# Replacing a seven-product feed-forward by plain three-product matmuls of 512 columns, with one weight pool from the RWKV readout on

## The chip, the cores and the metric

The kernel runs on one core of a Trainium2 chip, as one launch. The metric is the device time of that launch in microseconds. TensorE is called PE below, its weight loads PEld, VectorE DVE, ScalarE ACT, GpSimd POOL, and SP is the engine that issues the DMAs.

## What is computed

The reference is a network of two blocks over 512 latent tokens and 256 context tokens of 1024 features. The first block has an attention and delta-net layer and a Hyena layer; the second has an attention layer and an RWKV layer, each followed by a SwiGLU feed-forward. The change touches the feed-forward behind the RWKV layer, which is the last step before the final norm. By then only the 512 latent tokens are left:

```python
def _swiglu(h, wg, wu, wd):
    return (jax.nn.silu(h @ wg) * (h @ wu)) @ wd
...
        h2 = _rmsnorm(x, norm2_g[i]) * (1.0 + m[:, 4]) + m[:, 3]
        x = x + m[:, 5] * _swiglu(h2, ffn_wg[i], ffn_wu[i], ffn_wd[i])
...
    return _rmsnorm(x, final_g)
```

`wg` and `wu` are 1024 x 2816 and `wd` is 2816 x 1024: in units of 128 features, 8 columns in, 22 columns hidden, 8 columns out.

## The kernel before

All activations are held feature-major: `self.x` is eight tiles of 128 features by 512 tokens. A float32 factor is split into a high and a low part in a rounded format (`hi`, a copy by ACT; `lo`, the difference, on POOL or DVE), and a float32 product is made of three matmuls, high by high, high by low and low by high, which add up in one PSUM bank (`mm3`, L189 to L193).

**The plain scheme** is `linear` (L195). It makes 128 output features: `load_w` (L178) has SP load one slab of the weights (`wraw`, two buffers), ACT makes `whi` (L172) and POOL makes `wlo` (L168; three buffers each), and per chunk of 128 of the contraction `mm3` issues its three matmuls. A column of `wg` or `wu` has 8 chunks, so 24 matmuls. The first feed-forward (`ffn`, L1482 onwards) uses it for 512 latent and 256 context tokens side by side: for each hidden column a column of `wg` and one of `wu`, Silu on ACT (L1507), the product on DVE (L1511), and the split of the result on ACT and POOL; the hidden columns come in groups of 8, 8 and 6, and after each group eight columns of `wd` add what it gives to `x` (`residual`, L1321). The eight output columns of the RWKV readout (`rwkv_out`) use `linear` for the latent tokens alone.

**The seven-product scheme** is `ffn_s` (L381). It takes weights and activations as 2 x 2 blocks and forms two output columns by 512 tokens from seven block products of 256 columns in place of eight, as in Winograd's form of Strassen's multiplication. `strassen` (L314) loads two slabs (L326), forms sums and differences of weight blocks on DVE (`total`, L336, four a call), splits seven blocks (`form`, L291 on ACT and L292 on POOL or DVE), runs the seven products, and combines them from PSUM on DVE (L359, L362, L363, L366) with one copy on ACT (L352). `sums` (L304) forms and splits the sums of activation blocks (L310 to L312). The first pair of columns goes by eight products (`eight`, L367) while the sums of the inputs are still being made. The hidden pairs come in groups of 4, 6, 6 and 6 columns, and the `wd` columns of a group are issued behind the first pair of the next.

**Around it.** `rwkv_out` ends with the eight columns of `rw_wo`; each adds to `x` and counts its squares (L232 on ACT, L234 on DVE, and behind the last column two matmuls L236), and behind the eighth the norm factor `r` follows on ACT (L209, L210). The feed-forward begins with that factor. `finish` scales `x` by the last norm factor (L2036 on ACT, L2037 on DVE and POOL) and stores eight tiles (L2038).

What sets the order: at build time a planner lays out the instructions of each engine by program order and by its own estimate of when operands and buffers are ready, and each engine and each DMA queue then works in that fixed order. A tile waits until all readers of the tile that held its space are done. The weight pool `w1` of the readout is closed before the feed-forward opens its own pools in the same space, which hold 176 KB per partition. `norm_mod` (L246) is the plain scheme's norm: per chunk a product on DVE (L255), the high part on ACT (L262), the shifted value on DVE (L263) and the low part on POOL (L168).

```python
        nc.tensor.matmul(ps, lhsT=a[0], rhs=b[0], start=start, stop=False)
        nc.tensor.matmul(ps, lhsT=a[0], rhs=b[1], start=False, stop=False)
        nc.tensor.matmul(ps, lhsT=a[1], rhs=b[0], start=False, stop=stop)
```

Of the kernel before, what the change touches and what calls it, by code (L numbers as in the profile page):

```python
# [10 lines left out]
F32 = mybir.dt.float32  # L11
# [6 lines left out]
L = 512  # L18
C = 256

# name -> number of 128-feature columns
# [17 lines left out]
_FFG = [[8, 8, 6], [4, 6, 6, 6]]  # L39
# [13 lines left out]
def nat_i(ap):  # L53
    """(column, row) tokens, seen as (row, column)."""
    return ap.rearrange("p (c r) -> p r c", r=8)
# [6 lines left out]
class K:  # L62
# [38 lines left out]
    @contextmanager  # L101
    def phase(self, name, side="left", **tags):
        """tag -> (bufs, columns); the enclosing phases' tags stay."""
        outer = getattr(self, "pb", None), getattr(self, "tags", {})
        with self.tc.tile_pool(name=name, bufs=1, side=side, reuse_waits="tile") as self.pb:
            self.tags = {**outer[1], **{t: (self.pb, *n) for t, n in tags.items()}}
            yield
        self.pb, self.tags = outer

    @contextmanager  # L110
    def psum(self, name, **tags):
        """tag -> bufs, or (bufs, banks)."""
# [13 lines left out]
    def halves(self, name, dt=F32):  # L126
        """an endless supply of [128, 256], two to a tile."""
        while True:
            t = self.k2(name, dt)
            yield t[:, 0:256]  # L130
            yield t[:, 256:512]
# [26 lines left out]
    def table(self, i):  # L158
        """loads an activation table; ScalarE's instructions of the block stay behind it."""
# [6 lines left out]
    def ptt(self, out, in0, in1, op):  # L166
        """a tensor_tensor on GpSimd."""
        self.nc.gpsimd.tensor_tensor(out=out, in0=in0, in1=in1, op=op)  # L168

    def split(self, src, hi, lo, psum=False):  # L170
        """float32 = hi + lo, both in the rounded format."""
# [23 lines left out]
    def linear(self, src, acts, evac, kc=8, late=False, w=None):  # L195
        """128 outputs. acts: list of (list of (hi, lo) per K chunk, n); evac(a, psum)."""
# [7 lines left out]
    def rstd(self, ps, n, scale, eps, name="rstd", bias=0.0, table=False, out=None):  # L204
        """exp(bias) (ps scale + eps)^-1/2"""
# [7 lines left out]
    def sumsq(self, tiles, n):  # L213
        """tiles: [128, 512], 512 / n chunks each; -> sums over all of them, on all partitions."""
# [10 lines left out]
    def count(self, key, c, src, n, scale=1.0, tag="ss"):  # L225
        """adds the squares of column c of 8; -> their sum with the last one."""
# [12 lines left out]
    def squares(self, a, c, n, tag="ss"):  # L239
        """counts column c in the norms of x (a = 0) or ctx; with the last one they are in self.rr[a]."""  # L240
# [4 lines left out]
    def norm_mod(self, tiles, n, g, sh, name, table=False, tag="k2", r=None):  # L245
        """(x rstd) g + sh, split; g, sh: [128, 8] columns."""  # L246
# [28 lines left out]
    def mod(self, w, chunks, outs):  # L275
        """outs: list of (silu(c) rows, out columns tile, chunks below which it is wanted)."""
# [12 lines left out]
    def split_on(self, vector, src, hi, lo):  # L289
        """split, the difference on VectorE or GpSimd."""  # L290
        self.nc.scalar.copy(hi, src)  # L291
        (self.nc.vector if vector else self.nc.gpsimd).tensor_tensor(out=lo, in0=src, in1=hi.bitcast(F32), op=ALU.subtract)  # L292
        return hi, lo

    def operand(self, ts, n, tag):
        """ts: [128, 4 n] each, the blocks 22 11 21 12 of right operands' chunks: rows of the first | second half of the
        contraction, columns of the first | second half of the tokens. -> the split factors of the seven products."""
        hl = [[self.sb(tag, tag + x, F32R)[:, :7 * n] for x in "hl"] for _ in ts]
        for t, (h, l) in zip(ts, hl):
            self.split_on(False, t[:, :3 * n], h[:, 0:3 * n], l[:, 0:3 * n])  # L300
        return self.sums(ts, n, hl)

    def sums(self, ts, n, hl):
        nc = self.nc  # L304
        tt = nc.vector.tensor_tensor
        for t, (h, l) in zip(ts, hl):
            s = self.sb("sT", "sT")[:, :4 * n]
            b = t.rearrange("p (a n) -> p a n", a=4)
            # T1 | T3, T2 | -T4
            tt(out=s[:, 0:2 * n].rearrange("p (a n) -> p a n", a=2), in0=b[:, ::-3], in1=b[:, 1::2], op=ALU.subtract)  # L310
            tt(out=s[:, 2 * n:3 * n], in0=t[:, 0:n], in1=s[:, 0:n], op=ALU.subtract)
            tt(out=s[:, 3 * n:4 * n], in0=t[:, 2 * n:3 * n], in1=s[:, 2 * n:3 * n], op=ALU.subtract)  # L312
            self.split_on(True, s[:, 0:2 * n], h[:, 3 * n:5 * n], l[:, 3 * n:5 * n])
            self.split_on(False, s[:, 2 * n:], h[:, 5 * n:], l[:, 5 * n:])  # L314
        return [{k: (h[:, i * n:i * n + n], l[:, i * n:i * n + n]) for i, k in enumerate(("22", "11", "21", "T1", "T3", "T2", "T4"))} for h, l in hl]

    def strassen(self, srcs, acts, n, kc=8, plain=False):
        """2 x 128 outputs (srcs: their columns of the weights), 2 n tokens, seven products for eight (Winograd's form).
        acts: operand() per chunk of half the contraction; -> [128, 4 n], blocks in the order of operand()."""
        nc = self.nc  # L320
        m = kc // 2
        w = 128 * m
        raw = []
        for src in srcs:
            raw.append(self.sb("wr", "wraw"))
            nc.sync.dma_start(raw[-1][:, :2 * w], src)  # L326
        A = {f"{i + 1}{j + 1}": raw[i][:, j * w:j * w + w] for i in range(2) for j in range(2)}

        def form(k, vector):
            hi, lo = (self.sb("w" + x, "w" + x, F32R)[:, :w] for x in ("fh", "fl"))  # L330
            self.split_on(vector, A[k], hi, lo)
            return [t.rearrange("p (k m) -> p k m", k=m) for t in (hi, lo)]

        def total(k, a, b, op, out=None):
            A[k] = A[out] if out else self.sb("ws", "wsum")[:, :w]
            nc.vector.tensor_tensor(out=A[k], in0=A[a], in1=A[b], op=op)  # L336

        def product(ps, a, b, vector=False):
            f = form(a, vector)
            for k in range(m):  # L340
                self.mm3(ps, [t[:, k, :] for t in f], acts[k][b], k == 0, k == m - 1)

        if plain:
            return self.eight(form, acts, n)
        p1 = self.bank("mm", "pst")[:, :n]
        x, y, z = (self.bank("mm", "pst")[:, :2 * n].rearrange("p (a n) -> p a n", a=2) for _ in range(3))
        o = self.sb("so", "so")[:, :4 * n]
        o4 = o.rearrange("p (a n) -> p a n", a=4)
        tt = nc.vector.tensor_tensor
        bc = lambda t: t.unsqueeze(1).to_broadcast([128, 2, n])  # L350
        product(p1, "11", "11")
        nc.scalar.copy(o4[:, 1], p1)  # L352
        total("S1", "21", "22", ALU.add)
        total("S3", "11", "21", ALU.subtract, "21")
        total("S2", "S1", "11", ALU.subtract, "11")
        product(x[:, 1], "12", "21")
        total("S4", "12", "S2", ALU.subtract, "12")
        product(x[:, 0], "S2", "T2")
        tt(out=o4[:, 0:2], in0=x, in1=bc(o4[:, 1]), op=ALU.add)  # L359
        product(y[:, 1], "S1", "T1", True)  # L360
        product(y[:, 0], "S3", "T3")
        tt(out=o4[:, 2:4], in0=y, in1=bc(o4[:, 0]), op=ALU.add)  # L362
        tt(out=o4[:, 0], in0=y[:, 1], in1=o4[:, 2], op=ALU.add)  # L363
        product(z[:, 1], "S4", "22")
        product(z[:, 0], "22", "T4")
        tt(out=o4[:, 2:4], in0=z, in1=o4[:, 2:4], op=ALU.add)  # L366
        return o  # L367

    def eight(self, form, acts, n):
        """strassen() by the eight products."""  # L370
        o = self.sb("so", "so")[:, :4 * n]
        o4 = o.rearrange("p (a n) -> p a n", a=4)
        f = {k: form(k, k[0] == k[1]) for k in ("11", "12", "21", "22")}
        for slot, i, j in ((1, 1, 1), (2, 2, 1), (0, 2, 2), (3, 1, 2)):
            ps = self.bank("mm", "pst")[:, :n]
            for q in (1, 2):
                for k, a in enumerate(acts):
                    self.mm3(ps, [t[:, k, :] for t in f[f"{i}{q}"]], a[f"{q}{j}"], q == 1 and k == 0, q == 2 and k == len(acts) - 1)
            self.nc.scalar.copy(o4[:, slot], ps)
        return o  # L380

    def ffn_s(self, i, ml, mc, g, groups):
        """the same for x alone, seven products for eight."""
        nc, A = self.nc, self.A
        n = 256
        ts, hl = [], []
        for c in range(4):
            t = self.sb("sh", "nm")[:, :1024]
            h, l = (self.sb("sx", "sx" + x, F32R) for x in "hl")
            b, hb = (a.rearrange("p (a n) -> p a n", n=n) for a in (t, h))  # L390
            ts.append(t)
            hl.append((h, l))
# [1897 lines left out]
```

## Time and profile before

| what | value |
|---|---|
| times of three runs | 3710.51, 3719.08 and 3720.9 us |
| median of the runs | 3719.08 us |
| profiled execution, first to last instruction | 3710.4 us |
| mean granted TensorE clock over it | 0.912 of full speed |
| PE, DVE, POOL, ACT busy over it | 85%, 66%, 55%, 42% |
| last feed-forward: first to last matmul start | 3235.5 to 3690.2 us |
| first feed-forward, dense part | 1661.6 to 2190 us |

The profiled execution is as long as the fastest of the three runs, to 0.1 us; the median stands 8.6 us above it. Times in the trace count from the first instruction. A share of busy time is a mean over stages that have different limits, so that the stage of the change is read by itself. PEclk is the granted clock: 1.00 is 2.4 GHz and 0.50 is 1.2 GHz. The duration of a matmul includes its passage through the array; how often one starts is read from the starts of neighbours.

### The profile page before, as it was taken

Reading aid. Unit: us, or ns where it says so; the run is one execution under the profiler, and the core shown is the slowest. Engines: PE = TensorE matmul, PEld = TensorE weight load, DVE = VectorE, ACT = ScalarE, POOL = GpSimd, SP = SyncE. Lnnn points to the kernel's source line nnn. Section 1 sums busy time; section 2 is a strip of 40 time slices with the busy share of each in tenths; the row PEclk is TensorE's granted clock in tenths of the full one; section 3 lists DMA queues with packets and bytes.
Section 4 is the critical chain, followed back from the end, with each engine's and each line's share of the span. In section 5 each row is a group of like instructions: output and inputs, shape, how many; then the busy total and the mean of one; then the engine's idle time right before and its main releaser. Section 6 shows DMA issues by size and latency. Waiting matters only on the chain. (4 is left out here: it accounts for less than half of the span.)

```text
span 3710.4 us, 56859 instructions
## 1 busy us (share of the span) xinstructions
PE 3144.4 (85%) x21442; PEld 2555.7 (69%) x21442; DVE 2457.0 (66%) x3749; ACT 1547.8 (42%) x3033; POOL 2050.1 (55%) x1855
## 2 busy tenths in 40 slices
PE   5678896889997889999999996898667787788887
PEld 1257675767876677778888885666556666488886
DVE  7977844547775676570532339565788885689987
ACT  3347542443222456632121133563545554343434
POOL 6742531446665555434333336467468871488886
PEclk9889996999998899999999997799778988899998
DMA  6312358733441431032343421454322324212221
GB/s 212 119 63 80 134 196 242 211 122 124 134 139 44 130 103 35 19 125 63 114 148 114 136 86 59 163 211 146 96 61 78 81 75 126 83 57 83 83 86 63
DMA packets 266633, 412.37 MB, mean 111 GB/s; under 512 B 73844, under 2 KB 155380, under 8 KB 266360
## 3 DMA queue, kind: packets, MB, share of 16 engines
q1 hardware_dynamic: 266360, 408.75, 35.1%
q8 instruction: 169, 2.77, 0.3%
q14 instruction: 104, 0.85, 0.1%
HBM read 331.34 MB, written 70.25 MB: 108 GB/s over the span
## 5 line engine op out<-in xcount | busy, mean ns | idle before, releaser
L168 POOL TENSOR_TENSOR wlo<-wraw,whi 128x1024 fp32r<-128x1024 f32 (+1 forms) x204 | 506.3, 2484 | 728.1 <-ACT whi L172 705.5
L172 ACT CAST whi<-wraw 128x1024 fp32r<-128x1024 f32 (+1 forms) x204 | 211.5, 1039 | 606.3 <-PE pmm L192 504.4
L191 PE MATMUL pmm<-hxh,whi 128*128 128x512 f32 x968 | 391.7, 406 | 11.2 <-ACT hxh L262 6.5
L192 PE MATMUL pmm<-hxl,whi 128*128 128x512 f32 x968 | 389.1, 402 | 13.2 <-POOL hxl L168 13.2
L284 DVE SCALAR_TENSOR_TENSOR mjunk<-mraw,cv 128x1024 bf16<-128x1024 f32 x224 | 358.7, 1601 | 61.6 <-DMA mraw<-in_mod_w 36.9
L193 PE MATMUL pmm<-hxh,wlo 128*128 128x512 f32 x968 | 387.6, 401 | 0.0
L292 POOL TENSOR_TENSOR wfl<-wraw,wfh 128x512 fp32r<-128x512 f32 (+2 forms) x220 | 306.4, 1422 | 83.8 <-ACT wfh L291 79.9
L191 PE MATMUL pmm<-hch,whi 128*128 128x256 f32 x760 | 222.0, 292 | 9.4 <-ACT hch L262 6.7
L192 PE MATMUL pmm<-hcl,whi 128*128 128x256 f32 x760 | 221.5, 291 | 8.1 <-POOL hcl L168 8.0
L192 PEld LDWEIGHTS pmm<-hxl,whi 128*128 128x128 f32 x968 | 184.1, 190 | 57.4 <-POOL hxl L168 18.8
L191 PEld LDWEIGHTS pmm<-hxh,whi 128*128 128x128 f32 x968 | 184.3, 191 | 53.9 <-ACT hxh L262 9.0
L193 PE MATMUL pmm<-hch,wlo 128*128 128x256 f32 x760 | 221.2, 291 | 0.0
L193 PEld LDWEIGHTS pmm<-hxh,wlo 128*128 128x128 f32 x968 | 184.2, 190 | 40.9 <-issue 0.7
L914 POOL TENSOR_TENSOR X<-X,binv 128x30 f32<-128x30 f32 (+4 forms) x330 | 195.9, 594 | 23.7
L913 POOL TENSOR_TENSOR binv<-X 128x30 f32<-128x30 f32 (+4 forms) x330 | 192.4, 584 | 24.0
L193 PE MATMUL pst<-sxh,wfl 128*128 128x256 f32 x608 | 182.4, 302 | 27.1 <-POOL wfl L292 16.7
L191 PE MATMUL pst<-sxh,wfh 128*128 128x256 f32 x608 | 181.5, 299 | 11.5 <-ACT wfh L291 11.2
L192 PE MATMUL pst<-sxl,wfh 128*128 128x256 f32 x608 | 178.8, 294 | 3.4 <-POOL sxl L398 3.4
L291 ACT CAST wfh<-wraw 128x512 fp32r<-128x512 f32 (+2 forms) x224 | 117.8, 560 | 150.9 <-DVE wraw L336 126.0
L191 PE MATMUL pmm<-lh,whi 128*128 128x512 f32 (+1 forms) x360 | 134.0, 378 | 38.6 <-ACT lh L1579 19.1
L191 PEld LDWEIGHTS pmm<-hch,whi 128*128 128x128 f32 x760 | 149.0, 196 | 18.3 <-ACT hch L262 8.5
L192 PEld LDWEIGHTS pmm<-hcl,whi 128*128 128x128 f32 x760 | 148.8, 196 | 16.8 <-POOL hcl L168 11.6
(599 smaller groups left out, 9288.4 us busy)
## 6 DMA issues: line engine op xcount, KB each, us to landing
mraw<-in_mod_w SPq DMA_DIRECT2D x96, 512.0 KB, 3.6
wraw<-in_wg SPq DMA_DIRECT2D x44, 512.0 KB, 3.6
wraw<-in_wu SPq DMA_DIRECT2D x44, 512.0 KB, 3.6
wraw<-in_e_w_in SPq DMA_DIRECT2D x32, 512.0 KB, 3.8
wraw<-in_o_w_in SPq DMA_DIRECT2D x32, 512.0 KB, 3.5
mraw<-in_e_mod_w SPq DMA_DIRECT2D x24, 512.0 KB, 4.0
mraw<-in_o_mod_w SPq DMA_DIRECT2D x24, 512.0 KB, 4.1
wraw<-in_wd SPq DMA_DIRECT2D x32, 384.0 KB, 3.1
```

Source lines behind the costliest of these rows:

```text
L168: self.nc.gpsimd.tensor_tensor(out=out, in0=in0, in1=in1, op=op)
L172: self.nc.scalar.copy(hi, src)
L191: nc.tensor.matmul(ps, lhsT=a[0], rhs=b[0], start=start, stop=False)
L192: nc.tensor.matmul(ps, lhsT=a[0], rhs=b[1], start=False, stop=False)
L193: nc.tensor.matmul(ps, lhsT=a[1], rhs=b[0], start=False, stop=stop)
L284: nc.vector.scalar_tensor_tensor(out=junk, in0=raw, scalar=1.0, in1=cv, op0=ALU.mult, op1=ALU.mult, accum_out=out[:, c:c + 1])
L291: self.nc.scalar.copy(hi, src)
L292: (self.nc.vector if vector else self.nc.gpsimd).tensor_tensor(out=lo, in0=src, in1=hi.bitcast(F32), op=ALU.subtract)
L913: tt(out=tv, in0=v[:, k + 1:, k:k + 1].to_broadcast(sh), in1=v[:, k:k + 1, :k].to_broadcast(sh), op=ALU.mult)
L914: tt(out=v[:, k + 1:, :k], in0=v[:, k + 1:, :k], in1=tv, op=ALU.add)
```

## The change

The second feed-forward is computed by `ffn`, the function of the first, called with the latent tokens alone: `ffn(1, ...)` leaves the context out of `acts`. The functions of the seven-product scheme go. The hidden columns of the second feed-forward are grouped 8, 8, 6 instead of 4, 6, 6, 6. The pool `w1`, opened for the readout's weights, stays open until the end and also holds the feed-forward's `wraw`, `whi` and `wlo`. The feed-forward's other tiles come from 52 buffers of 512 columns (104 KB per partition), and it has six PSUM banks for products instead of seven. The diff also removes comments and docstrings, which moves the line numbers.

```diff
-_FFG = [[8, 8, 6], [4, 6, 6, 6]]
+_FFG = [[8, 8, 6], [8, 8, 6]]
...
-    def split_on(self, vector, src, hi, lo):
...
-    def operand(self, ts, n, tag):
...
-    def sums(self, ts, n, hl):
...
-    def strassen(self, srcs, acts, n, kc=8, plain=False):
...
-    def eight(self, form, acts, n):
...
-    def ffn_s(self, i, ml, mc, g, groups):
...
-                self.linear(A[f"wd0{gi}"][c], [(hid[a], n) for a, (_, n) in enumerate(acts)], dev, kc=nf, late=True)
+                self.linear(A[f"wd{i}{gi}"][c], [(hid[a], n) for a, (_, n) in enumerate(acts)], dev, kc=nf, late=True)
...
-            t = self.sb("sx", "fin")[:, :L]
+            t = self.k2("fin")
...
-    with k.weights("w1"), k.phase("ro", "right", ld=(16, 512)), k.phase("rc", "right", k2=(40, 512)), k.psum("ps_out", mm=2, pp=2, p=3, ss=1):
-        k.rwkv_out(m[0])
-    with k.phase("f1", k2=(2, 512), ws=(2, 512), sT=(1, 1024), so=(3, 1024), sx=(8, 1792), sh=(8, 1792), wr=(4, 1024), wfh=(6, 512), wfl=(6, 512)), k.psum("ps_f1", mm=7, ss=1):
-        k.ffn_s(1, *m, _FFG[1])
-        k.finish(out)
+    with k.weights("w1"):
+        with k.phase("ro", "right", ld=(16, 512)), k.phase("rc", "right", k2=(40, 512)), k.psum("ps_out", mm=2, pp=2, p=3, ss=1):
+            k.rwkv_out(m[0])
+        with k.phase("f1", k2=(52, 512)), k.psum("ps_f1", mm=6, ss=1):
+            k.ffn(1, *m)
+            k.finish(out)
```

## Rows read from the trace of the kernel before

**Rows 1.** Busy us (instructions) by engine, clock, DMA share, GB/s: the last feed-forward.
```profile
3235.00:3692.00 457.00, 388.80 (x2796) 368.30 (x2796) 410.88 (x447) 191.75 (x380) 363.64 (x254) 0.91 0.24 73
```

**Rows 2.** PE's timeline, the last 256-column matmuls: start, duration.
```profile
3690.11 0.28 PE L192 MATMUL pst<-shl,wfh 128*128 128x256 f32 x1
3690.23 0.28 PE L193 MATMUL pst<-shh,wfl 128*128 128x256 f32 x1
```

**Rows 3.** Waits, 3262 to 3692: total us, times, longest.
```profile
ACT wfh L291 <- DVE wraw L336: 126.0, 34, 7.8
POOL wfl L292 <- ACT wfh L291: 59.9, 43, 4.1
...
PEld pst L193 <- POOL wfl L292: 25.9, 37, 2.0
```

**Rows 4.** DVE's timeline, residuals of two neighbouring columns of the readout.
```profile
3212.68 0.75 DVE L1321 SCALAR_TENSOR_TENSOR x<-pmm,ml,x 128x512 f32<-128x512 f32 x1 [1.70 <-PE pmm L193]
...
3218.26 0.75 DVE L1321 SCALAR_TENSOR_TENSOR x<-pmm,ml,x 128x512 f32<-128x512 f32 x1 [1.68 <-PE pmm L193]
```

**Rows 5.** As rows 1: the first feed-forward, dense part.
```profile
1661.60:1700.00 38.40, 38.40 (x205) 33.26 (x205) 9.65 (x17) 14.53 (x21) 25.44 (x16) 0.95 0.14 43
1700.00:2190.00 490.00, 489.98 (x2787) 427.82 (x2786) 155.84 (x217) 99.92 (x145) 184.53 (x99) 1.00 0.35 113
```

**Rows 6.** DMA issues of the page: count, KB each, median us to landing.
```profile
wraw<-in_wg SPq DMA_DIRECT2D x44, 512.0 KB, 3.6
...
wraw<-in_wd SPq DMA_DIRECT2D x32, 384.0 KB, 3.1
```

**Rows 7.** Costliest groups, 1700 to 2190: busy us, mean ns, idle before.
```profile
L168 POOL TENSOR_TENSOR wlo<-wraw,whi 128x1024 fp32r<-128x1024 f32 x53 | 133.8, 2524 | 253.3 <-ACT whi L172 253.3
...
L172 ACT CAST whi<-wraw 128x1024 fp32r<-128x1024 f32 x53 | 55.6, 1049 | 281.6 <-PE pmm L192 256.8 <-DMA wraw<-in_wu 23.6 <-DMA wraw<-in_wg 1.1
...
L168 POOL TENSOR_TENSOR hl<-sg,hh 128x512 fp32r<-128x512 f32 x20 | 25.8, 1292 | 1.6 <-ACT hh L172 1.6
...
L1511 DVE TENSOR_TENSOR sg<-sg,pmm 128x512 f32<-128x512 f32 x20 | 13.8, 688 | 93.6 <-PE pmm L193 92.5 <-ACT sg L1507 1.1
L172 ACT CAST hh<-sg 128x512 fp32r<-128x512 f32 x20 | 12.4, 621 | 4.4 <-DVE sg L1511 4.1
L1507 ACT ACTIVATE sg<-pmm 128x512 f32<-128x512 f32 x20 | 11.9, 593 | 0.0
```

**Rows 8.** ACT's timeline, the last squares of the readout and its norm factor.
```profile
3230.20 0.63 ACT L232 ACTIVATE sq<-x 128x512 f32<-128x512 f32 x1 [4.94 <-DVE x L1321]
...
3232.86 0.63 ACT L210 ACTIVATE r<-r 128x512 f32<-128x512 f32 x1
```

**Rows 9.** DVE and ACT timelines, the norm of the first feed-forward, two chunks.
```profile
1658.44 0.68 DVE L255 TENSOR_TENSOR nm<-x,r 128x512 f32<-128x512 f32 x1
...
1659.16 0.81 ACT L262 ACTIVATE hxh<-nm,ml,gx 128x512 fp32r<-128x512 f32 x1 [1.12 <-DVE nm L255]
...
1660.46 0.68 DVE L255 TENSOR_TENSOR nm<-x,r 128x512 f32<-128x512 f32 x1
```

**Rows 10.** As rows 1: the last feed-forward's first 26.5 us.
```profile
3235.50:3262.00 26.50, 15.12 (x60) 13.36 (x61) 25.86 (x26) 10.83 (x20) 19.16 (x12) 0.51 0.20 60
```

**Rows 11.** DVE's timeline, the final products at the end of the kernel.
```profile
3700.41 5.83 DVE L2037 TENSOR_TENSOR fin<-fin,r 128x512 f32<-128x512 f32 x6 [5.25 <-ACT r L210]
```

**Rows 12.** PE's timeline, the last matmul of the readout's last column.
```profile
3228.98 0.40 PE L193 MATMUL pmm<-roh,wlo 128*128 128x512 f32 x1
```

**Rows 13.** SP's timeline, the first weight loads of the last feed-forward.
```profile
3228.71 0.80 SPq L326 DMA_DIRECT2D wraw<-in_wg  x2
```

**Rows 14.** PE's waits in the readout, 3180 to 3230: total us, times, longest.
```profile
PE pmm L191 <- ACT roh L172: 2.7, 1, 2.7
PE pmm L192 <- POOL rol L168: 1.0, 1, 1.0
PE pmm L191 <- DVE x L1321: 0.3, 1, 0.3
```

More of the change, by code (lines that the diff above doesn't have):

```diff
@@ L287, in mod_tile @@
         return (pool or self.pm).tile([128, n], F32, name=name)
-    def split_on(self, vector, src, hi, lo):
-        self.nc.scalar.copy(hi, src)
-        (self.nc.vector if vector else self.nc.gpsimd).tensor_tensor(out=lo, in0=src, in1=hi.bitcast(F32), op=ALU.subtract)
-        return hi, lo
-    def operand(self, ts, n, tag):
[L298 to L301, printed above, removed]
@@ L303, in sums @@
-    def sums(self, ts, n, hl):
[L304 to L315, printed above, removed]
@@ L317, in strassen @@
-    def strassen(self, srcs, acts, n, kc=8, plain=False):
[L320 to L367, printed above, removed]
@@ L369, in eight @@
-    def eight(self, form, acts, n):
[L371 to L380, printed above, removed]
@@ L382, in ffn_s @@
-    def ffn_s(self, i, ml, mc, g, groups):
[L384 to L392, printed above, removed]
-            for k, o, d in ((c, b[:, 1::2], hb[:, 1:2]), (c + 4, b[:, 2::-2], hb[:, 2::-2])):
-                col = g["x2"][:, k:k + 1], ml[:, 24 + k:25 + k]
-                nc.vector.tensor_tensor(out=o, in0=self.x[k].rearrange("p (a n) -> p a n", n=n), in1=self.rr[0].rearrange("p (a n) -> p a n", n=n), op=ALU.mult)
-                nc.scalar.activation(out=d, in_=o[:, :d.shape[1]], func=AF.Identity, scale=col[0], bias=col[1])
-                nc.vector.tensor_scalar(out=o, in0=o, scalar1=col[0], scalar2=col[1], op0=ALU.mult, op1=ALU.add)
-            nc.gpsimd.tensor_tensor(out=l[:, :768], in0=t[:, :768], in1=h[:, :768].bitcast(F32), op=ALU.subtract)
-        more = [self.sb("sh", "b12" + x, F32R).rearrange("p (a n) -> p a n", n=n) for x in "hl"]
-        for c in range(4):
-            self.split_on(False, ts[c][:, 768:], more[0][:, c], more[1][:, c])
-        acts = self.sums(ts, n, hl)
-        first = [{**a, "12": (more[0][:, c], more[1][:, c])} for c, a in enumerate(acts)]
-        def up(f0, f, nf):
-            pair = (f0 + f, f0 + f + nf // 2)
-            plain = pair[0] == 0
-            sg = self.strassen([A["wg"][i, q] for q in pair], first if plain else acts, 256, 8, plain)
-            nc.scalar.activation(out=sg, in_=sg, func=AF.Silu)
-            t = self.strassen([A["wu"][i, q] for q in pair], first if plain else acts, 256, 8, plain)
-            nc.vector.tensor_tensor(out=t, in0=t, in1=sg, op=ALU.mult)
-            return self.operand([t], 256, "sh")
-        def down(gi, hid):
-            for c in range(0, 8, 2):
-                t = self.strassen([A[f"wd1{gi}"][c + q] for q in range(2)], hid, 256, 2 * len(hid))
-                b = t.rearrange("p (a n) -> p a n", a=4)
-                for q, o in enumerate((b[:, 1::2], b[:, 2::-2])):
-                    x = self.x[c + q].rearrange("p (a n) -> p a n", a=2)
-                    self.residual(x, o, ml[:, 40 + c + q:41 + c + q])
-                    if gi == len(groups) - 1:
-                        self.squares(0, c + q, L)
-        late = None
-        for gi, nf in enumerate(groups):
-            hid = []
-            for f in range(nf // 2):
-                hid.extend(up(sum(groups[:gi]), f, nf))
-                if late and f == 1 - 1:
-                    down(*late)
-            late = gi, hid
-        down(*late)
```

## The prediction

> **What bounds the kernel now.** I first read the whole page, which shows PE busy for 85% of the span, and then cut the span by stage, because that share mixes stages with different limits. The stage that the change replaces runs from the first matmul of the last feed-forward at 3235.5 us to its last one, which starts at 3690.2 us [rows 1, 2]: 455 us with 2796 matmuls of 256 columns. Neighbouring matmuls start 0.12 us apart where PE has nothing to wait for [rows 2], so the stage holds 2796 x 0.12 = 335.5 us of matmuls at the full clock. The other 119 us are waits and stretches at a lower clock. In the same window DVE is busy for 411 us and POOL for 364 us of 457 [rows 1]. The waits say how they hold PE up: ACT waits 126 us for DVE's sums and differences of weight blocks, POOL waits for ACT, and PE waits for the split weights [rows 3]. So this stage is bound by the chain DVE, ACT, POOL that prepares the seven-product factors, with PE behind it. It ends the kernel, so what it loses or gains comes straight off the span, as long as the readout before it and the tail behind it keep their lengths.
>
> **The matmuls of the new stage.** The change needs 44 columns of `wg` and `wu` with 24 matmuls each, and 8 columns of `wd` per group with 24, 24 and 18: 44 x 24 + 16 x 24 + 8 x 18 = 1584 matmuls of 512 columns in 68 weight columns. Their price is in the readout, which already runs `linear` with 512 latent tokens alone: the residuals of neighbouring columns start 5.58 us apart [rows 4], and 5.58 / 24 = 0.2325 us. The new stage thus holds 1584 x 0.2325 = 368.3 us of matmuls, 33 us more than now: the plain scheme does 8/7 of the products, and longer matmuls win back only part of it. As a test of the figure, the first feed-forward alternates 512 and 256 columns, so that a pair should take 0.2325 + 0.12 = 0.3525 us; 2787 matmuls in 490 us make 0.352 [rows 5].
>
> The Trainium skill (TensorE: Matmul & The Clock Gate, "Back-to-back issue gap") gives N / 2.4 + 2.5 ns between starts, 216 ns at 512 columns. By that the sum would be 1584 x 0.216 = 342 us; the trace has 0.2325 us for this form of matmul, and that is used.
>
> **Can weights be fed at that pace?** Each column needs one DMA of 512 KB (3.6 us to landing; 3.1 us for the small ones [rows 6]), a cast on ACT of 1.05 us and a difference on POOL of 2.5 us [rows 7]. Two `wraw` buffers turn over in 3.6 + 1.05 + 2.5 = 7.15 us each, one column every 3.6 us against PE's 5.58. Per hidden column (two weight columns, 11.16 us of PE) POOL has 2 x 2.52 + 1.29 = 6.3 us, ACT 2 x 1.05 + 0.62 + 0.59 for Silu = 3.3 us, DVE 0.69 us [rows 7]. DVE, now the busiest, nearly falls out. The first feed-forward shows the same helpers with PE busy for 489.98 of 490 us at a granted clock of 1.00, and ACT there mostly waits for PE to give weight buffers back [rows 5, 7]; it has more PE time per column, since the context tokens share the weights, but the margin above covers that. SP's queue has nothing but these loads until the final stores. I take no wait for weights in the steady part.
>
> **Where it is not steady.** The start: `r` is ready at 3233.5 us [rows 8]. The first chunk's high part then needs what it needed in the first feed-forward, 0.72 us from DVE's start to ACT's and 0.81 us for ACT [rows 9], so the first matmul can start at 3233.5 + 0.1 + 0.72 + 0.81 = 3235.1, say 3235.2. That is when it starts now. Chunks follow every 2.02 us [rows 9], eight in about 16 us. Meanwhile three columns of weights can be ready, if the longer-lived pool lets them load during the readout: 72 matmuls, or 16.7 us. So PE has work while the chunks arrive, provided the planner interleaves the columns. Four losses, each with both ends:
> - PE idles between readout and feed-forward and so begins at 1.2 GHz. In the first feed-forward the clock came to 0.95 over 38.4 us of unbroken work [rows 5], a loss of 0.05 x 38.4 = 2 us; now the start of the last one stays at 0.51 for all of 26.5 us, with PE in use for 15 [rows 10]. If the whole chunk stretch of 16 us ran at the half clock it would lose 8. I take 3, near the first, because PE will have three columns to chew on.
> - Chunks come later than in the first feed-forward if DVE is given all eight products first, and weights four to six must be split as the first three finish together: 0 to 8 us, I take 1.5, since the same function shows 38.4 us of 38.4 busy just behind its start [rows 5].
> - The seam from the hidden columns to `wd`, three times: the last hidden column needs 0.69 + 0.62 + 1.29 = 2.6 us [rows 7] plus up to 1.05 + 2.5 us if weight work stands ahead of it on ACT and POOL. The first `wd` column covers it with its earlier chunks, 21 matmuls or 4.9 us (15 or 3.5 us in the last group). That leaves 0 to about 2 us a seam, 0 to 6 in all; I take 2.
> - The pool that stays open puts casts and splits of the feed-forward's first weights into the readout. One cast of 1.05 us may stand on ACT ahead of the last squares at 3230.20 [rows 8]: 0 to 1.05 us, I take 0.5. A gain can't come from there, since the norm factor and not the weights starts the stage.
>
> Together 7 us, between 2 and 23.
>
> **The tail.** Now the last matmul starts at 3690.23 [rows 2], and combining the products, two residuals, and squares lie between it and `r`; DVE's first final product starts at 3700.41 [rows 11], and the span ends at 3710.4. The new tail looks like the end of the readout: last matmul start 3228.98 [rows 12], `r` complete at 3233.49 [rows 8], 4.5 us, or 4.3 us after the 0.2325 of that matmul are counted. From `r` to the end nothing changes: 10 us. So 14.3 us behind the matmuls against 20.2 now, less the 0.12 of the last one.
>
> **The sum.** 3235.2 + 368.3 + 7.0 + 14.3 = 3624.8 us for the profiled execution, against its 3710.4: 85.6 us less, or 2.3%. Everything ahead of the readout's last columns keeps its code and its place. The profiled execution lies at the fastest of the runs; the median is 3719.1, and 3719.1 - 85.6 = 3633 us is the forecast.
>
> **The rivals.**
> - *The prefetch does not happen.* If the planner, or a tile of the readout, holds the first weights back until the readout is over, as now, when the first one leaves at 3228.7 us [rows 13], the first column's low part comes 7.15 us behind the load. For it: the load needs a `wraw` buffer that the readout's own eight columns use too. Against: two buffers turn over well ahead of PE [rows 6, 7]. Price about 5 us: 3638.
> - *The stage keeps losing time by the column, as the readout does.* PE waited 2.7 + 1.0 + 0.3 = 4.0 us over the eight columns of the readout [rows 14]. Over 68 columns that is 34 us: 3667. Against: these waits are for the readout's own activations at its first column, and the first feed-forward has none in 490 us [rows 5].
> - *Slower: weights one column at a time.* If the load, the cast and the split of a column did not overlap those of the next (a buffer given back only behind a later wait on POOL or on SP's queue), a column would take 7.15 us and a small one 3.1 + 0.75 x (1.05 + 2.5) = 5.8 [rows 6, 7]; 60 x 7.15 + 8 x 5.8 = 475 us in place of 368.3, so 107 us more: 3740, slower by 0.6%. It decides from a mean of (368.3 + 85.6) / 68 = 6.7 us a column on. For it: PE's waits now are for weights too [rows 3]. Against: 5.58 us a column in the readout [rows 4].
> - *Shorter spacing.* If 512 columns took 0.216 us, as spacing without weight changes might, the matmuls would come to 342 us: 26 us less, 3607. Against: every dense stretch read here gives 0.2325 [rows 4, 5]. This is the rule of the Trainium skill named above (TensorE: Matmul & The Clock Gate).
>
> **How the numbers follow.** The forecast's own mechanism, PE-bound at the readout's pace, has 0.73; the missing prefetch 0.08, the loss by column 0.10, the shorter spacing 0.05, the slower rival 0.04. With the losses between 2 and 23 us the forecast's own range is 3628 to 3649 on the median, and 3620 to 3649 if the run falls at the fast end of the 8.6 us between runs. To hold 8 in 10 the range reaches to the loss by column above and to the shorter spacing below: 3606 to 3670. A measurement of this kernel can tell about 0.3%, 11 us, from no change. All cases but the slower rival lie more than 40 us below 3719; of the slower one a quarter would fall near no change: faster 0.95, same 0.01, slower 0.04.
>
> **What would show it.** Right: 1584 matmuls of 512 columns in the last stage, starts 0.2325 us apart, PE busy over 97% of it at a granted clock near 1.00 behind the first 20 us, DVE busy under 60 us in it, ACT's casts waiting for PE, the loads of the first weights issued before 3229 us, last matmul near 3610 and 14.3 us from there to the end. Wrong: PE waiting for `wlo` or `whi` in the steady part, a spacing other than 0.2325, a first stretch of over 20 us at half clock, or a readout that ends later than now.

## The result, and the profile after

The changed kernel takes 3627.14 us, the median of four runs (3620.37 to 3628.45), against 3717.70 us for four runs of the kernel before (3710.51 to 3720.90). The ratio is 0.9758, with a 95% interval of 0.9745 to 0.9772: 90.6 us less, where 85.6 were forecast (3633 us).

The profiled execution took 3628.29 us, and its span is 3626.5 us. The head of its page, the span and the busy time, share and instructions of each engine:

```profile
span 3626.5 us, 53156 instructions
PE 3127.6 (86%) x20230; PEld 2496.3 (69%) x20230; DVE 2086.7 (58%) x3364; ACT 1462.3 (40%) x2785; POOL 1887.3 (52%) x1699
```

The shares over the whole span barely tell what happened: PE goes from 85% to 86%. The stage does. This is the view of busy time by engine, with granted clock, DMA share and GB/s, of the last feed-forward as a whole, of four stretches of it, and of a piece of the first feed-forward:

```profile
3239.00:3612.00 373.00, 366.54 (x1588) 300.81 (x1588) 49.93 (x68) 105.01 (x130) 191.24 (x95) 0.99 0.27 88
3240.00:3247.00 7.00, 6.16 (x14) 4.39 (x15) 4.31 (x8) 2.45 (x4) 5.21 (x4) 0.52 0.04 16
3247.00:3265.00 18.00, 15.88 (x68) 12.48 (x67) 4.96 (x9) 8.15 (x10) 11.74 (x7) 0.97 0.06 20
3264.10:3267.70 3.60, 3.60 (x10) 2.83 (x9) 0.00 (x0) 1.23 (x2) 3.07 (x3) 0.53 0.56 174
3265.00:3600.00 335.00, 335.00 (x1474) 277.39 (x1473) 37.47 (x47) 88.72 (x109) 174.29 (x86) 1.00 0.29 95
1710.00:2160.00 450.00, 450.00 (x2559) 393.25 (x2558) 141.35 (x204) 89.59 (x128) 172.09 (x92) 1.00 0.35 116
```

Against [rows 1] DVE fell from 411 us to 50 in the stage, and the 1584 matmuls (and four of the norm) fill PE for 366.5 of 373 us. Between 3265 and 3600 PE has no gap at all: 335.00 of 335 us at a granted clock of 1.00. All the loss lies in the first 28 us. The clock is at 0.52, near its lower level of 1.2 GHz, for the first 7 us, where it was at 0.51 for 26.5 [rows 10], and it is there once more, at 0.53, for 3.6 us from 3264.1 on.

The waits of the stage turned round. These are those from 3262 to 3612, as in [rows 3]; the columns are the engine and what it waited for, total us, times and longest:

```profile
ACT whi L172 <- PE pmm L192: 213.8, 53, 7.9
...
POOL wlo L168 <- ACT whi L172: 159.7, 60, 5.8
...
PE pmm L191 <- ACT whi L172: 2.1, 1, 2.1
```

Before, ACT waited for DVE's sums and PE for the weights [rows 3]. Now ACT waits 213.8 us for PE to give weight buffers back, and PE has waited for weights once.

PE's timeline (start, duration) at the start of the stage, at its first refill, in the steady part and at the end:

```profile
3240.06 1.53 PE L191 MATMUL pmm<-hxh,whi 128*128 128x512 f32 x3 [3.11 <-ACT hxh L262]
3242.37 0.79 PE L192 MATMUL pmm<-hxl,whi 128*128 128x512 f32 x1 [0.78 <-POOL hxl L168]
...
3243.39 0.63 PE L192 MATMUL pmm<-hxl,whi 128*128 128x512 f32 x1
3243.82 0.63 PE L193 MATMUL pmm<-hxh,wlo 128*128 128x512 f32 x1
...
3260.82 0.39 PE L192 MATMUL pmm<-hxl,whi 128*128 128x512 f32 x1
3263.32 0.50 PE L191 MATMUL pmm<-hxh,whi 128*128 128x512 f32 x1 [2.11 <-ACT whi L172]
...
3264.54 0.63 PE L192 MATMUL pmm<-hxl,whi 128*128 128x512 f32 x1
3264.97 0.63 PE L193 MATMUL pmm<-hxh,wlo 128*128 128x512 f32 x1
...
3267.53 0.41 PE L193 MATMUL pmm<-hxh,wlo 128*128 128x512 f32 x1
...
3300.44 0.39 PE L193 MATMUL pmm<-hxh,wlo 128*128 128x512 f32 x1
...
3301.12 0.39 PE L193 MATMUL pmm<-hxh,wlo 128*128 128x512 f32 x1
...
3607.12 0.40 PE L193 MATMUL pmm<-hh,wlo 128*128 128x512 f32 x1
...
3609.02 1.13 PE L236 MATMUL pss<-sq,cst 128*128 128x512 f32 x2 [0.64 <-ACT sq L232]
```

Three matmuls in 3301.12 - 3300.44 = 0.68 us are 0.2267 a piece, and that is the steady spacing; at the half clock they start 0.43 apart. Ahead of 3263.32 the three columns that were ready have been used up, the fourth has just begun, and the weights come 2.1 us late. Behind that wait, from 3264.1 on, the starts are 0.43 apart once more, until 3267.53.

ACT's timeline around the norm factor that starts the stage, and at the end of the kernel:

```profile
3234.17 1.04 ACT L172 CAST whi<-wraw 128x1024 fp32r<-128x1024 f32 x1 [3.97 <-PE pmm L192]
3235.14 0.63 ACT L232 ACTIVATE sq<-x 128x512 f32<-128x512 f32 x1
...
3237.80 0.63 ACT L210 ACTIVATE r<-r 128x512 f32<-128x512 f32 x1
...
3608.34 0.63 ACT L232 ACTIVATE sq<-x 128x512 f32<-128x512 f32 x1 [3.46 <-DVE x L1177]
3608.99 1.28 ACT L161 ACT_TABLE_LOAD   x1
3610.28 5.00 ACT L1892 ACTIVATE fin<-x,cols 128x512 f32<-128x512 f32 x8
3615.19 0.67 ACT L209 ACTIVATE r<-pss,eps 128x512 f32<-128x512 f32 x1
```

The cast of a prefetched weight at 3234.17 is over as the squares can start. `r` is ready at 3237.80 + 0.63 = 3238.43, and PE begins 1.63 us later. At the end, eight products of `finish` (5.00 us) stand on ACT ahead of the norm factor, though the sum of squares that it needs is there at 3609.02 + 1.13 = 3610.15. Only then come DVE's final products. Here is DVE's timeline of them, to be set beside [rows 11], and SP's timeline of the feed-forward's first loads, to be set beside [rows 13]:

```profile
3616.55 5.83 DVE L1893 TENSOR_TENSOR fin<-fin,r 128x512 f32<-128x512 f32 x6 [8.25 <-ACT r L210]
```

```profile
3215.43 0.33 SPq L183 DMA_DIRECT2D wraw<-in_wg  x1
3221.00 0.33 SPq L183 DMA_DIRECT2D wraw<-in_wu  x1
3226.58 0.33 SPq L183 DMA_DIRECT2D wraw<-in_wg  x1
```

Three weight columns were asked for 23, 17 and 12 us ahead of `r`, during the readout.

**Where the time came from**, in us, from these rows and [rows 2, 8, 12]:

| part | before | after | change |
|---|---|---|---|
| span's start to `r` | 3233.49 | 3238.43 | +4.9 |
| `r` to first matmul | 2.0 | 1.63 | -0.4 |
| first to last matmul start | 454.8 | 367.1 | -87.7 |
| last matmul start to end | 20.2 | 19.4 | -0.8 |
| span | 3710.4 | 3626.5 | -83.9 |

The first line is not the change's. In two of the runs below whose code ahead of the readout's last columns is the same (experiment 1, and 512 bytes in experiment 6), `r` came at 3235.2 and 3243.0, and the difference arises in the attention layer, between about 510 and 810 us. Why that stretch varies is open. So runs are compared below by the **stage**, from `r` to the end of the span: 476.9 us before, 388.1 after.

### The profile page after: what moved, and what is told of

Its sections match the earlier page's. It is cut to its first block, busy times and chain, and to the rows that moved or that the text cites. A ratio compares the mean times of both kernels' runs of the same rounds, so it can differ in the third digit from the quotient of the medians.

```text
span 3626.5 us, 53156 instructions
## 1 busy us (share of the span) xinstructions
PE 3127.6 (86%) x20230; PEld 2496.3 (69%) x20230; DVE 2086.7 (58%) x3364; ACT 1462.3 (40%) x2785; POOL 1887.3 (52%) x1699
## 5 line engine op out<-in xcount | busy, mean ns | idle before, releaser
L168 POOL TENSOR_TENSOR wlo<-wraw,whi 128x1024 fp32r<-128x1024 f32 (+1 forms) x272 | 665.8, 2450 | 897.5 <-ACT whi L172 868.9
L172 ACT CAST whi<-wraw 128x1024 fp32r<-128x1024 f32 (+1 forms) x272 | 281.2, 1036 | 863.2 <-PE pmm L192 738.4
L191 PE MATMUL pmm<-hxh,whi 128*128 128x512 f32 x1320 | 529.6, 404 | 16.8 <-ACT hxh L262 9.4
L192 PE MATMUL pmm<-hxl,whi 128*128 128x512 f32 x1320 | 529.1, 401 | 12.6 <-POOL hxl L168 12.6
L193 PE MATMUL pmm<-hxh,wlo 128*128 128x512 f32 x1320 | 527.0, 400 | 0.0
L191 PEld LDWEIGHTS pmm<-hxh,whi 128*128 128x128 f32 x1320 | 252.3, 191 | 74.9 <-ACT hxh L262 12.3
L193 PEld LDWEIGHTS pmm<-hch,wlo 128*128 128x128 f32 x760 | 149.1, 196 | 1.5 <-issue 0.8
L1696 PE MATMUL pgB<-W,BK 128*64 128x192 f32 (+1 forms) x768 | 108.1, 358 | 45.8 <-ACT B L1699 25.8
L191 PE MATMUL pmm<-hh,whi 128*128 128x512 f32 x352 | 137.9, 392 | 0.0
L192 PE MATMUL pmm<-hl,whi 128*128 128x512 f32 x352 | 137.8, 392 | 0.0
```

The source lines that it names most:

```text
L1696: nc.tensor.matmul(view(p)[half[q], a], lhsT=bk[:, a0 + a, hh, o:o + 64], rhs=rhs, start=True, stop=True)
```

## The experiments

**1. Without the prefetch.** The first two slabs of the feed-forward are held back until the norm factor is there, by a one-column copy from it into the slab's buffer ahead of the load.

```diff
+        if self.hold:
+            self.hold -= 1
+            nc.scalar.copy(raw[:, :1], self.rr[0][:, :1])
...
+            k.hold = 2
             k.ffn(1, *m)
```

> The changed kernel, but the loads of the first two weight columns of the last feed-forward must wait for the norm factor r (one element of it is copied into their buffers first). Theory that the pool kept open is worth only a start: from r to the first matmul 1.6 us become about 5 us (a load of 3.4 us, a cast of 1.05 us), PE's waits in the stage grow by 3 to 7 us, and the stage from r to the end grows by as much, 388 to about 393 us. Rival, that the weights loaded ahead carry a good part of the 90 us: the stage grows by 20 us or more.

Measured: 3631.44 us (3629.70 to 3634.43), ratio to before 0.9767 [0.9752, 0.9781]. The stage is 393.6 us, 5.5 longer. SP's timeline shows the first load leave as `r` is ready (3235.18 here), and ACT's the cast it feeds:

```profile
3235.49 0.33 SPq L186 DMA_DIRECT2D wraw<-in_wg  x1
```

```profile
3239.41 1.04 ACT L172 CAST whi<-wraw 128x1024 fp32r<-128x1024 f32 x1 [2.65 <-DMA wraw<-in_wg]
```

The first matmul, in PE's timeline, starts 5.3 us behind `r` and not 1.6:

```profile
3240.50 0.80 PE L194 MATMUL pmm<-hxh,whi 128*128 128x512 f32 x1 [6.81 <-ACT whi L172]
```

So the prefetch is worth about 5 us. By the code, it is the pool that spans both stages that makes room for it; no run closes that pool.

**2. The plain scheme with 256 columns.** `linear` runs the two halves of the tokens one after the other in the last feed-forward: twice the matmuls at half the width, with the same weights, so that each block of weights is loaded into PE twice.

```diff
-            for k in range(kc):
-                self.mm3(ps[:, :n], [t[:, k, :] for t in w], act[k], k == 0, k == kc - 1)
+            for s in (slice(0, 256), slice(256, 512)) if self.narrow else (slice(0, n),):
+                for k in range(kc):
+                    self.mm3(ps[:, s], [t[:, k, :] for t in w], [t[:, s] for t in act[k]], k == 0, k == kc - 1)
```

> The changed kernel with each matmul of the last feed-forward cut into two of 256 columns (first one half of the tokens for all chunks, then the other): 3168 matmuls, all else as it is. Theory that PE's spacing sets the stage: 3168 x 0.12 = 380 us of matmuls in place of 1584 x 0.2273 = 360, so about 20 us more (3647), PE still busy all through, and still some 70 us faster than the kernel before: the long matmuls are worth a fifth of the gain, dropping the block sums the rest. Rival, that PE has slack in the new stage: no change. Rival, that the long matmuls carry the gain: 60 us or more back.

Measured: 3646.16 us (3644.34 to 3650.76), ratio to before 0.9808 [0.9792, 0.9824]; the stage is 409.2 us, 21 longer. The view by engine of 300 us of the steady part:

```profile
3270.00:3570.00 300.00, 300.00 (x2503) 300.00 (x2502) 24.40 (x34) 72.85 (x88) 147.77 (x71) 1.00 0.31 92
```

300 / 2503 = 0.1199 us a matmul, PE full again. Two of them cost 0.240 against 0.227 for one of 512. The new stage is bound by PE alone, and about 21 of the 89 us that it saves are owed to the width.

**3. The seven products without DVE's weight sums.** In the kernel before, `total` hands on its first block and adds nothing; the loads, splits, seven products and their combination stay. This kernel leaves out a part of the computation and serves only to price it.

```diff
-            A[k] = A[out] if out else self.sb("ws", "wsum")[:, :w]
-            nc.vector.tensor_tensor(out=A[k], in0=A[a], in1=A[b], op=op)
+            A[k] = A[a]
```

> The kernel before, with the 144 sums and differences of weight blocks left out (the products then use the plain blocks, so part of the computation is missing). Theory that the chain from DVE through ACT and POOL bound the old stage: with some 150 us less on DVE, and no in-place sums that wait for POOL, PE's waits shrink and the stage from the first to the last matmul falls from 455 to between 380 and 420 us, towards the 335 us of its matmuls. Rival, that the old stage was held by PE itself or by its clock: 440 us or more.

Measured: 3627.16 us (3626.27 to 3628.57), ratio 0.9761 [0.9744, 0.9777], as fast as the changed kernel. From first to last matmul start it takes 369.1 us, and the stage 390.0. By engine, and ACT's largest wait from 3262 to 3600:

```profile
3235.00:3605.00 370.00, 349.39 (x2790) 344.39 (x2791) 283.67 (x303) 202.42 (x381) 345.02 (x254) 0.96 0.29 91
```

```profile
ACT wfh L291 <- PE pst L192: 88.8, 129, 2.5
```

ACT's 126 us of waiting for DVE's sums [rows 3] are gone, it waits for PE instead, and PE is busy for 349 of 370 us. The gain was expected too small: of the 119 us that the old stage took beyond its matmuls, 454.8 - 369.1 = 86 us hang on these sums. With them at no cost, seven products of 256 columns would only draw level with eight of 512.

**4. The final products in one operation.** In `finish` of the changed kernel, `x` is multiplied by the gain and by `r` in one DVE operation.

```diff
-            nc.scalar.mul(t, self.x[c], self.col("final_g", c))
-            (nc.gpsimd if c in (2, 5) else nc.vector).tensor_tensor(out=t, in0=t, in1=r, op=ALU.mult)
+            nc.vector.scalar_tensor_tensor(out=t, in0=self.x[c], scalar=self.col("final_g", c), in1=r, op0=ALU.mult, op1=ALU.mult)
```

> The changed kernel with the final scaling as one DVE instruction per column, x times final_g times r, in place of a product on ACT and one on DVE or POOL. Theory that the tail is longer than forecast because eight products on ACT (5.0 us) stand ahead of the norm factor's Ln in ACT's order: Ln starts about 5 us earlier behind the last squares, the tail from the last matmul's start to the end falls from 19.4 to about 14.7 us, and the run is 4 to 5 us shorter. Rival, that Ln waits for the two matmuls that sum the squares: no change of the tail.

Measured: 3622.13 us (3616.78 to 3625.99), ratio to before 0.9740 [0.9725, 0.9754]; the stage is 381.3 us, 6.8 shorter. From the last matmul start to the end it takes 13.3 us in place of 19.4. ACT's and DVE's timelines:

```profile
3603.55 1.28 ACT L161 ACT_TABLE_LOAD   x1
3604.84 0.69 ACT L209 ACTIVATE r<-pss,eps 128x512 f32<-128x512 f32 x1
```

```profile
3606.22 5.39 DVE L1892 SCALAR_TENSOR_TENSOR fin<-x,cols,r 128x512 f32<-128x512 f32 x8 [3.36 <-ACT r L210]
```

The norm factor follows the table load at once. It starts 3.2 us behind the last matmul's start (3601.68 in this run) in place of 8.1: the eight products on ACT had held the end back by 4.9 us. The other 1.2 us of the shorter tail lie behind `r`, where one operation does the work of two.

**5. One raw weight buffer.** The last feed-forward's `wraw` has one buffer in place of two, so that a column's load must wait for the split of the one before.

```diff
-        raw = self.pw.tile([128, 1024], F32, name="wraw", tag="wraw", bufs=2)
+        raw = self.pw.tile([128, 1024], F32, name="wraw", tag="wraw1" if self.one else "wraw", bufs=1 if self.one else 2)
```

> The changed kernel with one buffer for the raw weights of the last feed-forward in place of two, so that the load of a column waits for the split of the one before. Theory of the slower rival's price: a column then takes 3.4 + 1.05 + 2.45 us and some 0.3 us of hand-over, 7.2 us (the small ones 5.8) instead of 5.46 on PE: 60 x 7.2 + 8 x 5.8 = 478 us of stage in place of 367, and the run comes out 15 to 25 us slower than the kernel before. Rival, that the order of the loads leaves slack that this sum misses: a stage under 420 us.

Measured once: 3736.70 us, beside 3717.29 for the kernel before; first to last matmul start 472.6 us. Its waits from 3262 to 3700:

```profile
ACT whi L172 <- DMA wraw<-in_wd: 110.5, 22, 6.1
...
ACT whi L172 <- DMA wraw<-in_wg: 94.9, 20, 6.0
...
PE pmm L193 <- POOL wlo L168: 77.8, 59, 1.7
```

ACT waits for nearly every load and PE for nearly every low part. This is the slower rival made real, and its price of 475 us was right. Without the overlap of load, cast and split from column to column the change would be no gain.

**6. Moving the tiles by 640, 512 and 64 bytes.** The steady spacing of 0.2267 was not the readout's 0.2325. In the program as built, the weight tiles and the moving tiles of the last feed-forward start at addresses per partition that leave the same remainder by 512; in the first feed-forward and the readout the difference leaves 384. So a pad is put ahead of the last feed-forward's tiles. It was run with 160 elements of four bytes (640 bytes; the difference leaves 384), 128 (512 bytes; it leaves 0 again) and 16 (64 bytes; 448):

```diff
-        with k.phase("f1", k2=(52, 512)), k.psum("ps_f1", mm=6, ss=1):
+        with k.phase("pad", pad=(1, 160)), k.phase("f1", k2=(52, 512)), k.psum("ps_f1", mm=6, ss=1):
+            k.nc.vector.memset(k.sb("pad", "pad"), 0.0)
```

640 bytes:

> The changed kernel with a pad of 640 bytes per partition ahead of the feed-forward's tiles, so that their addresses leave 2016 instead of 1376 when divided by 2048, as those of the readout and of the first feed-forward do; the weights' addresses leave 1376 in all three. Theory that this offset between the moving tiles and the weights sets the spacing (0.2273 us in the last feed-forward, 0.2325 in the other two): the spacing goes to about 0.2325 us and the stage grows by 8 us. Rival, that addresses have no part in it: 0.2273 us and no change.

512 bytes:

> The changed kernel with a pad of 512 bytes ahead of the last feed-forward's tiles. Theory that the remainder by 512 of the distance between weights and moving tiles sets the spacing: the distance keeps its remainder of 0, and the spacing stays at 0.2265 to 0.2275 us. Rival, that any shift of the tiles, or the pad itself, lengthens it: about 0.233 us as with 640 bytes.

64 bytes:

> The changed kernel with a pad of 64 bytes ahead of the last feed-forward's tiles: the distance between weights and moving tiles then leaves 448 by 512. Theory that only a remainder of 0 is fast: the spacing goes to 0.231 to 0.235 us and the stage from r to the end from 388 to about 397 us, as with 640 bytes. Rival, that small distances don't matter and 640 bytes are a bad case of their own: 0.2265 us and 388 us.

The same 300 us of the steady part by engine, for 640 bytes, 512 bytes and 64 bytes in turn:

```profile
3270.00:3570.00 300.00, 300.00 (x1287) 241.38 (x1286) 25.11 (x35) 76.77 (x92) 151.44 (x74) 1.00 0.29 94
```

```profile
3270.00:3570.00 300.00, 300.00 (x1320) 248.37 (x1319) 25.77 (x36) 79.03 (x95) 157.35 (x77) 1.00 0.30 98
```

```profile
3270.00:3570.00 300.00, 300.00 (x1310) 246.24 (x1310) 25.08 (x35) 77.80 (x93) 157.10 (x75) 1.00 0.29 97
```

300 us over the counts are 0.2331, 0.2273 and 0.2290 us, against 0.2262 without a pad, where the same window counts 1326 (a few records can be missing from a count). From the first to the last matmul start, which no count enters, it takes 376.6, 367.2 and 369.8 us, against 367.1. With 640 bytes the stage is 397.6 us, 9.5 longer, and the kernel 3632.60 us (3628.62 to 3637.47), ratio to before 0.9770 [0.9755, 0.9784]. With 512 bytes, the same extra instruction and nearly the same pad, it is 388.2 us, as without one (one run, 3632.95 us, with `r` late at 3243.0). With 64 bytes it is 390.8 us (one run, 3635.70): in between, which neither side had expected. So where the tiles lie sets the pace, and by degrees, not all or nothing. One rival is left: only the moving tiles were moved, and the weights' own addresses leave 352 by 512 in all these runs, so whether the distance counts or the moving tiles' own address is not shown.

**7. Both gains together.** Experiment 4's `finish`, and pads that bring the distance to 0 in other stages: 640 bytes ahead of the first feed-forward and of the readout, 160 bytes ahead of the Hyena layer and of the second part of the attention (`k.pad` opens a pool of one tile and sets it on POOL).

```diff
-        with k.phase("f0", "right", k2=(56, 512)), k.psum("ps_ffn", mm=6, ss=2):
+        with k.pad(160, "right"), k.phase("f0", "right", k2=(56, 512)), k.psum("ps_ffn", mm=6, ss=2):
...
-        with k.phase("ro", "right", ld=(16, 512)), k.phase("rc", "right", k2=(40, 512)), k.psum("ps_out", mm=2, pp=2, p=3, ss=1):
+        with k.pad(160, "right"), k.phase("ro", "right", ld=(16, 512)), k.phase("rc", "right", k2=(40, 512)), k.psum("ps_out", mm=2, pp=2, p=3, ss=1):
```

> The changed kernel with the fused final scaling and with pads that bring the moving tiles of the first feed-forward, the RWKV readout, the Hyena layer and the attention's output to the weights' remainder of addresses by 512, where the last feed-forward has it by chance. Theory that this remainder sets the spacing of 512-column matmuls: 0.2265 to 0.2275 us there in place of 0.2325, so 1584 x 0.006 = 9.5 us less in the first feed-forward, 1.2 us each in the readout and the attention's output, 0 to 5 us in the Hyena layer, where other engines bind too; with 6 us from the tail 18 to 23 us less than the changed kernel: about 3606. Rival, that only the last feed-forward reacts: 3621.

Measured: 3613.98 us (3610.31 to 3616.90), ratio to before 0.9723 [0.9706, 0.9740]; less than hoped for. The first feed-forward gained 7.3 us, and the Hyena layer lost 2.7. The spacing followed the pad in the Hyena layer too. PE's timelines of the changed kernel, where the distance leaves 160 there, and of this run, where it leaves 0, show three matmuls in 0.70 and in 0.68 us:

```profile
1000.17 0.40 PE L193 MATMUL pmm<-hxh,wlo 128*128 128x512 f32 x1
...
1000.87 0.40 PE L193 MATMUL pmm<-hxh,wlo 128*128 128x512 f32 x1
```

```profile
1020.20 0.39 PE L199 MATMUL pmm<-hxh,wlo 128*128 128x512 f32 x1
...
1020.88 0.39 PE L199 MATMUL pmm<-hxh,wlo 128*128 128x512 f32 x1
```

So what the layer lost, it lost elsewhere.

**8. The same without the pads at Hyena and attention.**

> The kernel of e7_best without the pads of the Hyena layer and of the attention's output. In e7_best the stretch from the Hyena layer's output weights to the attention's first was 121.4 us against 118.7 in nearly all other runs. Theory that the pad there costs this, with no gain: the stretch is 118.7 again, the first feed-forward stays at 575 us (582 without a pad), the tail at 13.3 us, and the run is 1 to 4 us under e7_best's 3614. Rival, that the 2.7 us are this run's own: the stretch differs again without a cause in the code, and the time is the same.

Measured: 3611.80 us (3611.01 to 3620.61), ratio to before 0.9722 [0.9707, 0.9737]. The Hyena layer is back at its old length. A stretch of the first feed-forward by engine:

```profile
1710.00:2160.00 450.00, 449.52 (x2589) 397.68 (x2588) 143.19 (x204) 90.80 (x130) 173.69 (x92) 1.00 0.35 116
```

It holds 30 matmuls more than the same 450 us of the changed kernel, which had 2559 (the kernel before has 2561): the effect of the address is there in a second stage. The first feed-forward is 5.4 us shorter and the stage 6.6, at 381.5. This version beats both kernels, by 15 us and by 104. From the version of experiment 7 its runs do not tell it apart.

## Why the prediction was right

The forecast of 3633 us was 6 us above the measured median. That median, 3627.14, lies 1 us below the range that the prediction gave its own mechanism on the median (3628 to 3649), and inside the whole range of 3606 to 3670. By its steps, in us:

| step | forecast | measured |
|---|---|---|
| `r` to first matmul | 1.7 | 1.63 |
| 1584 matmuls at the steady spacing | 368.3 (0.2325) | 359.1 (0.2267) |
| start and seams | 7.0 | 8.2 |
| behind the last matmul | 14.3 | 19.2 |
| stage | 391.3 | 388.1 |

**The bound.** Right. DVE's sums were the head of the chain that held the old stage (experiment 3), and PE is the bound of the new one (the windows; experiment 2). The weights are fed well inside the pace, as the sum from [rows 6, 7] had it.

**The spacing** is the one mis-sized term: 9.2 us too much. The prediction took the readout's 0.2325 [rows 4] as the price of the operation, and its test by the first feed-forward [rows 5] seemed to confirm it. But both stages have the same distance between weights and moving tiles, so they could not show that it matters. Experiment 6 gives 0.233 back in the new stage with that distance. The prediction's own list of what would show it wrong has "a spacing other than 0.2325", and that sign came. The trace of before could have told: in the first layer's input products, where the distance leaves 0, PE's timeline has three matmuls in 0.68 us.

```profile
253.82 0.39 PE L193 MATMUL pmm<-hxh,wlo 128*128 128x512 f32 x1
...
254.50 0.39 PE L193 MATMUL pmm<-hxh,wlo 128*128 128x512 f32 x1
```

**Start and seams.** Nearly right in sum, with other parts. 8.2 is what first to last start (367.1) and the last matmul's 0.23 leave over 359.1. The first three columns' 72 matmuls take from 3240.06 to about 3260.3, 20.2 us where 16.3 would do at the full pace. These 3.9 us are 0.8 of waiting for the first low part and some 3 of half clock, for which 3 were taken. The other 4.3 us came at the refill behind the third column, where 1.5 were taken with the chunks' order: 2.1 of waiting, and a second stretch at the half clock behind it, which the prediction had not thought of. The seams cost nothing where 2 were taken, since PE has no gap between 3265 and 3600. The cast ahead of the readout's last squares, for which 0.5 was taken, held them up by nothing that the trace shows.

**The tail** is the other mis-sized term: 4.9 us too little. "The new tail looks like the end of the readout" left out that at the end of the kernel eight products stand ready for ACT beside the norm factor. Experiment 4 shows that they cost all of it; why the planner put them first is open. In the kernel before, all eight stood ahead of the last squares on ACT, so its own tail did not show the danger. The errors, -9.2, +4.9 and +1.2, add up to 3 us on the stage. That two mis-sized terms cancel by more than half is luck, and the closeness of the sum is no proof of its terms.

**The rivals.** The missing prefetch was priced right (5 us; 5.5 measured) and did not occur. The loss by column, 34 us, did not either: PE's only wait for weights is the 2.1 us at the refill. The slower rival was priced at 475 us of matmuls, and the kernel that makes it real has 472.6. The shorter spacing came in part, 0.2267 and not 0.216. The rule of the Trainium skill named in the prediction (TensorE: Matmul & The Clock Gate, "Back-to-back issue gap"), which that section gives for an isolated matmul, is reached in none of these runs: the steady spacing of 512 columns is 0.2267 us at its shortest.

**Two readings that did not hold.** "Everything ahead of the readout's last columns keeps its code and its place": `r` came 4.9 us later than in the trace of before, and a readout that ends later was named as a sign of error; it is scatter from an earlier stage. And the profiled execution of before was taken for the fastest run because its span equals that run's time; but the profiled executions here take 1.8 us longer than their spans (3628.29 against 3626.5), so before's took about 3712. Neither changes the forecast, which is a difference.

## What to carry to other kernels

A scheme that saves products is paid for on the engine that forms the operands: here an eighth of the products was saved at the price of DVE work that held the stage up by 86 us, so ask which wait ends last before you count flops. Read the price of an operation from stages that differ in where their tiles lie, not only in what they compute, and look at the addresses when two stages of the same code differ by 2%. When a stage becomes the last one, look at what else is ready on each engine at its end, and not only at the chain that should come next.

## What had not been expected of the hardware

The pace of back-to-back matmuls of 512 columns with a weight load each depends on where the moving tile lies: 0.227 us when its distance per partition to the weights leaves 0 by 512 bytes, 0.229 at 448, 0.233 at 384, all with PE busy throughout at a granted clock of 1.00. The weights lay at the same remainder each time, so that it is the distance, and not the moving tile's own address, is a guess. The Trainium skill (SBUF — State Buffer, "Who interferes with whom") gives the matmul's moving operand and the weight loads read ports of their own, independent of each other; by that no such difference would be looked for, and these runs show one. What in the chip makes it is open, and so is whether 0 is the best remainder. Bringing it to 0 ahead of the Hyena layer shortened the spacing there too, but not the layer.
